# Bidirectional encoder trunk on one core: banks, places and order at the start of the retention stage

## The chip, the cores and the metric

The kernel runs on one core of one Trainium2 chip. The time is device microseconds of one execution; for the kernel before it is the median of three runs. Engines are named as in the profile: PE (TensorE matmul), PEld (its weight loads), DVE (VectorE), ACT (ScalarE), POOL (GpSimd), SP (SyncE, which issues most DMAs).

## The reference

Two groups of tokens (512 rows of 1024 each) pass through the same two layers, each of the form x + Mixer(RMSNorm(x)), and a final RMSNorm. The first mixer is differential attention, the second bidirectional retention. The part that matters here is the second:

```python
proj = h @ w_in                      # 1024 -> 2*1024 (q, k) + 2*2048 (values, gate)
q, k, v, gate = split(proj)
q, k = rotate(q), rotate(k) * RET_QK_DIM ** -0.5
o = retention(q, k, v, decay_fwd, True) + flip(retention(flip(q), flip(k), flip(v), decay_bwd, False))
o = rms_norm(o, subln_g, SUBLN_EPS).reshape(B, S, D_INNER) * silu(gate)
x = x + o @ w_out                    # 2048 -> 1024
```

There are 8 heads; q and k have 128 columns a head, values 256. One retention direction weights the scores q.k by a decay in the distance of the two rows, adds them up over the values of a chunk of 128 rows, and carries a state (k.v, decayed) from chunk to chunk. The kernel takes both directions together.

## The kernel before

**Arithmetic.** Every fp32 operand is split into a high and a low part (`hi_of` on ACT, `lo_of` on DVE, lines 469 to 473), and a product is made of three passes: high-high, high-low, low-high. The large matrix products use a scheme of seven products, named P1 to P7 and made in the order `SEQ` = P1, P2, P5, P6, P3, P7, P4; their partial results meet in three accumulators called x, y and z (line 42). P1, P5 and P2 open an accumulator; P6, P7 and P4 add to x, P3 adds to z. Between two of them ACT copies or DVE adds what stands in the accumulator so far, so P6 waits until P1 was copied, and so on.

**Stages.** The layer-1 projections, attention, the layer-2 projections (`projections`, line 855, over a list of `Unit`s), and then retention. The last layer-2 unit is a "wide" one that makes the values of heads 6 and 7; each of its products is four groups of twelve 128x256 matmuls (line 693). Its operands lie in numbered slots: P2's in slots 4 to 7, P1's in 0 to 3, P5's in 8 to 11, P6's in 26, 27, 14, 15. Its y accumulators take the two banks of tag `o` (5, 6), its z accumulators the two of tag `sc` (3, 4), its x accumulators two of the three of `pj` (0 to 2). `v_done` (line 813) splits each of its results and stores it to DRAM.

**Retention.** A block is a head of one group; there are 16, with four tiles of 128 rows each. `ahead(b, n)` prepares block b: `keys` (line 1594: split the keys, transpose them, L1603), two `score2` (L1623), `states` (L1643) and `queries`. Each takes a bank of tag `sc`. For each tile, `av2` (line 1669) makes the weighted sum with nine matmuls (L1679, L1683) in a bank of tag `o`; ACT squares it and takes a root (`norm_two`, lines 874 to 880), scales it (L896); PE turns it into the other half of the same bank (`turn_o`, L902); DVE multiplies it by the gate (`gate2`, L1336), which frees the bank. After two blocks of one group (a pair, counted p = 0 to 3, group g) the output product of that pair is owed: `out2` (line 1370) for two halves of rows r = 0, 1 with the seven products each (L1394), into the accumulators x (bank 0 for row 0, bank 7 for row 1), y (bank 1) and z (bank 2). `owe2` (line 1479) puts P1 of row 1 ahead of P4 of row 0. `evac_add` copies (L1433, L1450) or combines (L1438) the accumulators and adds the results to x in DRAM by an accumulating DMA from POOL (L970); the last pair adds to x in SBUF instead (`evac_last`, L1467). `w_split` (line 1313) loads one of the seven output weights of a pair (512 KB), from the weight matrix or from a sum `w1P` made earlier in DRAM, into one of two raw places and splits it (128x1024 on ACT and DVE).

**What sets the order.** Nothing runs when it is written. Every operation is put down in a plan with its engine, its cost, its reads and writes; `Plan.arrange` (line 141) then simulates the engines and writes out one order for each. PE takes operations in the order in which they were put down, within a window of 24; the others take what is due first, counted back from PE. A load counts as landed 2.0 + KB/200 us after its issue or later if the modelled bus is full (line 464), and is not issued more than 15 us before it is due. On the chip each engine then runs its list strictly in that order and waits at its head.

**The start of the retention stage** (lines 1701 to 1725). `LEFT` = 2 products of the last values unit (P7 and P4) are left when it begins. The loads of block 0 and its four `ahead` steps are put down, with the loads of block 1 after the first; the two products follow with tiles 0 and 1, and at tile 2 the seven `w_split`s of the first pair. Where everything lies is the table `LATE` (line 374): block 0 in the raw and staging places (raw0 to raw3, st0 to st2, os0), block 1 in slots 0 to 2 and 4 to 7.

**The last product** (P4 of row 1 of the last pair and group) is made in two halves of 256 columns (`part`, line 1397, matmuls L1401), each followed by its sum (L1408) and square (L1411).

Of the kernel before, what the change touches and what calls it, by code (L numbers as in the profile page):

```python
# [15 lines left out]
P = 128  # L16
S = 512
# [15 lines left out]
LEFT, LEFT1 = 2, 3  # L33
# [223 lines left out]
def trunk_kernel(  # L257
# [109 lines left out]
    def turns(kind, shape, dt=F32):  # L367
# [6 lines left out]
    LATE = dict(q0=["raw0"], k0=["raw1"], v0=["raw2", "raw3"], aT0=["st0", "st1"], kT0=["st2"], Z0=["os0"], sg0=["os1"], F0=[3],  # L374
                aT1=[0, 1], kT1=[2], Z1=["os2"], k1=[4], q1=[5], v1=[6, 7], AB=[8, 9, 10], sg1=[26], F1=[27], wa=[20], wb=[21], S4=[24],
                w=[11, 14, 15, 16, 17, 18, 19, "ws5", "ws6", 25, 12, 13, 22, 23],
                AS=["ws0", "ws1", "ws2", "ws3", "ws4"], O=["m1", "m2", "m3"], rt=["e0", "e1", "e2"], out=["e3", "e4", "e5", "e6", "e7"], R=["m0", "c3"],
                x=["raw0", "raw1", 20, 21, "raw2", "raw3", "os1", "os2"],
# [36 lines left out]
    BUFS = dict(pj=3, sc=2, o=2, tp=1, xs=1, x0=1, x1=1, y=1, z=1)  # L415
    BANKS = dict(pj=0, sc=3, o=5, tp=7, xs=3, x0=0, x1=7, y=1, z=2)
# [42 lines left out]
    def dma(out, in_, r, w, kb, eng=None, now=False):  # L459
# [4 lines left out]
        plan.op("SP" if eng is None else "ACT", 0.5, lambda: q.dma_start(out(), in_()), r, w, lands=2.0 + kb / 200.0,  # L464
                kb=kb, load=any(isinstance(k[0] if isinstance(k, tuple) else k, Buf) for k in w), now=now)

    last_store = [[]]
# [387 lines left out]
    def projections(units, early=None):  # L855

        if early is not None:
            units[2].early = early
        order = product_order(units)
        ready = 0  # L860
        for n, (u, op) in enumerate(order):
# [6 lines left out]
            u.product(op)  # L868
            u.evac(op)
            yield  # L870
# [148 lines left out]
    def units2(tab2):  # L1019
# [285 lines left out]
    def outputs(layer, xh, done):  # L1305
# [7 lines left out]
        def w_split(p, op):  # L1313

            src = w_d[layer, op, p] if (layer, op, p) in w_d else None
            t = late(("wa", "wb")[cnt_of.setdefault("raw", 0) % 2] + L, 0, [P, 2, S])
            cnt_of["raw"] += 1
            if src is None:
                e, i = W_BLOCK[op]
                dma(lambda: t.t, lambda: w_block(layer, p, e, i), [], [t], 512)  # L1320
            else:
                dma(lambda: t.t, lambda: src, [src], [t], 512)
            hi, lo = (late("w" + L, 2 * W_AT[op] + a, [P, 2, S], F32R) for a in range(2))
            hi_of(1024, lambda: hi.t, lambda: t.t, [t], [hi])
            lo_of(1024, lambda: lo.t, lambda: t.t, lambda: hi.t, [t, hi], [lo])
            wop[op] = (hi, lo)
# [43 lines left out]
        def out2(p, g, r, op):  # L1370
# [5 lines left out]
            if opens:  # L1376
                banks[which, r] = bank("xs" if which == "x" and ends and r else "x%d" % (r * layer) if which == "x" else which)
# [19 lines left out]
            def part(c):  # L1397
                at = slice(c * 256, c * 256 + 256)
                for i in range(2):
                    for n, (u, v) in enumerate(PASSES):  # L1400
                        nc.tensor.matmul(ps[:, at], pick(A[i], u), (hi, lo)[v][:, i, at], start=False,  # L1401
                                         stop=(i == 1 and n == 2), skip_group_check=True)
            if final:
                x, key = xh[g, 3][0]
                for c, own in enumerate(({}, {})):
                    at = slice(c * 256, c * 256 + 256)
                    pe(0.69, lambda c=c: part(c), [*A, hi, lo], [(ps, c)])
                    dve(256, lambda at=at: nc.vector.tensor_tensor(x()[:, at], x()[:, at], ps[:, at], op=ALU.add),  # L1408
                        [(ps, c), key], [own])
# [6 lines left out]
            pe(1.38, fn, [*A, hi, lo], [ps])  # L1416
# [153 lines left out]
    def fetch2(b):  # L1570
# [4 lines left out]
        dma(lambda: kf.t, lambda: k_src[h % 2], [k_src], [kf], 256)  # L1575
        dma(lambda: q.t.bitcast(F32), lambda: q_src[h % 2], [q_src], [q], 512)
        vt[b] = []
        for a in range(2):
# [3 lines left out]
                [src], [t], 512)  # L1582
# [7 lines left out]
    def decay(h):  # L1590
        t = Fs[h] = late(f"F{h % 2}", 0, [P, 2, S], F32R)
        dma(lambda: t.t.bitcast(F32), lambda: f_d[h][:], [f_d[h]], [t], 512)

    def keys(b):
# [4 lines left out]
        tp = bank("sc", "kT")  # L1599
# [14 lines left out]
    def score2(b, c):  # L1614
        h, g = blocks[b]
        s = bank("sc", "s2")
# [17 lines left out]
    def states(b):  # L1634
        z = bank("sc", "z2")
# [33 lines left out]
    def av2(b, t):  # L1669
        o = bank("o")  # L1670
# [31 lines left out]
    gate2, owe2, w_split = outputs(1, xh, final_norm)  # L1702
    fetch2(0)
# [107 lines left out]
```

## Time and profile before

| | us |
|---|---|
| median of three runs (lowest, highest) | 1833.79 (1831.55, 1835.36) |
| the profiled execution | 1829.8 |
| its span, first to last instruction | 1828.0 |
| PE busy | 1778.1 |
| DVE busy | 1485.2 |
| ACT busy | 1064.2 |

The profile is of one execution. Its page gives busy times, a row of 40 slices of the span, the chain of work that ended last, and groups of instructions by source line with the idle time before them. Views of the trace give the same for any stretch of time: busy time by windows, who waited for whom, the timeline. "L1679" is line 1679 of the kernel before. Tile names are those of the pools: `b` and `arena` are slots and places of the table above, `small` holds the keys of a block as loaded and the normed sums, `c` and `e` are copies and sums of accumulators.

### The profile page before, as it was taken

To read this page: it belongs to the slowest core of one execution; us is meant where nothing else is said; L and a number is where in the kernel's file an instruction comes from. 1 tells how busy PE (TensorE), PEld (TensorE's weight loads), DVE (VectorE), ACT (ScalarE), POOL (GpSimd) and SP (SyncE) were. 2 spreads that over 40 slices of the span, in tenths; PEclk is the share of its full clock that TensorE was granted. 3 is DMA by queue.
4 is the path that set the end of the run, shared out by engine and by line. 5 is a ranking of instruction groups with operands and counts; after the bars stand their busy time and mean duration, and the time that the engine had idled before them with its cause. 6 is when DMAs were issued, how large, how long until landed. Compare 5 with 4: busy or idle time off the path is not lost. (4 is left out here: it accounts for less than half of the span.)

```text
span 1828.0 us, 28378 instructions
## 1 busy us (share of the span) xinstructions
PE 1778.1 (97%) x10170; PEld 1532.2 (84%) x10170; DVE 1485.2 (81%) x2615; ACT 1064.2 (58%) x2278; POOL 240.6 (13%) x371
## 2 busy tenths in 40 slices
PE   7999999999999999999999999999999998999898
PEld 6988988988988878888888777989898897878776
DVE  7988888887888798888888897676766859778687
ACT  7644444444444486767677774444443458777674
POOL 3000000000000024443433100000000000121111
PEclk9999999999999999999999999999999999999999
DMA  8567667767766687878785457787765288889884
GB/s 289 166 182 200 199 187 200 213 174 204 209 175 185 237 294 220 244 232 249 233 246 185 139 168 235 208 243 209 228 195 168 98 273 266 232 221 257 225 244 138
DMA packets 197565, 387.04 MB, mean 212 GB/s; under 512 B 16432, under 2 KB 75440, under 8 KB 197296
## 3 DMA queue, kind: packets, MB, share of 16 engines
q1 hardware_dynamic: 174464, 342.95, 56.1%
q0 software_dynamic: 22528, 41.95, 14.4%
q8 instruction: 79, 1.29, 0.3%
q14 instruction: 62, 0.51, 0.1%
q10 hardware_dynamic: 432, 0.34, 0.1%
HBM read 250.96 MB, written 171.97 MB: 231 GB/s over the span
## 5 line engine op out<-in xcount | busy, mean ns | idle before, releaser
L645 PE MATMUL bank<-arena,ws 128*128 128x512 f32 x2202 | 527.2, 393 | 8.7 <-ACT ws L470 8.0
L645 PEld LDWEIGHTS bank<-arena,ws 128*128 128x128 f32 x2202 | 413.6, 189 | 100.6 <-ACT ws L470 8.0
L645 PE MATMUL bank<-b,ws 128*128 128x512 f32 x1170 | 290.8, 395 | 1.5 <-DVE e L722 1.5
L645 PEld LDWEIGHTS bank<-b,ws 128*128 128x128 f32 x1170 | 219.2, 188 | 52.7 <-DVE e L722 2.1
L1394 PE MATMUL bank<-b,b 128*128 128x512 f32 x794 | 212.6, 399 | 6.2 <-ACT c L1433 3.4
L470 ACT CAST ws<-st 128x512 fp32r<-128x512 f32 (+1 forms) x188 | 129.7, 694 | 135.5 <-PE bank L645 76.9
L693 PE MATMUL bank<-ws,arena 128*128 128x256 f32 x1728 | 205.0, 277 | 1.7 <-DVE e L803 1.7
L693 PEld LDWEIGHTS bank<-ws,arena 128*128 128x128 f32 x1728 | 201.4, 188 | 3.2 <-DVE e L803 1.9
L714 ACT COPY c<-bank 128x512 f32<-128x512 f32 x165 | 96.5, 585 | 174.7 <-PE bank L645 141.4
L473 DVE TENSOR_TENSOR ws<-st,ws 128x512 fp32r<-128x512 f32 (+1 forms) x188 | 145.4, 779 | 64.2 <-ACT ws L470 57.1
L1394 PEld LDWEIGHTS bank<-b,b 128*128 128x128 f32 x794 | 143.5, 188 | 35.6 <-ACT c L1433 3.9
L473 DVE TENSOR_TENSOR b<-b,b 128x512 fp32r<-128x512 f32 (+2 forms) x196 | 132.0, 686 | 19.0 <-ACT b L470 19.0
L722 DVE TENSOR_TENSOR e<-bank,c 128x512 f32<-128x512 f32 x165 | 113.7, 690 | 41.1 <-PE bank L645 34.2
L473 DVE TENSOR_TENSOR ws<-raw,ws 128x512 fp32r<-128x512 f32 (+1 forms) x143 | 109.8, 779 | 41.0 <-ACT ws L470 16.6
L970 POOL DMA_DIRECT2D x<-b x96 | 85.8, 903 | 376.6 <-DVE b L1438 253.4
L470 ACT CAST b<-b 128x512 fp32r<-128x512 f32 (+2 forms) x196 | 119.3, 621 | 24.6 <-DMA b<-w1P 8.1
L470 ACT CAST ws<-raw 128x512 fp32r<-128x512 f32 (+1 forms) x143 | 99.0, 698 | 56.5 <-PE bank L645 36.1
L693 PE MATMUL bank<-ws,b 128*128 128x256 f32 x960 | 118.8, 278 | 0.9 <-DVE e L722 0.9
L693 PEld LDWEIGHTS bank<-ws,b 128*128 128x128 f32 x960 | 114.7, 188 | 1.7 <-DVE e L722 1.1
L1243 ACT ACTIVATE b<-bank,nm 128x512 f32<-128x512 f32 x128 | 87.7, 687 | 35.0 <-DVE nm L1235 33.8
L1277 PE MATMUL bank<-arena 128*128 128x256 f32 x768 | 104.7, 286 | 0.2 <-DVE b L1336 0.2
L1227 PE MATMUL bank<-arena 128*128 128x512 f32 x384 | 101.8, 397 | 2.4 <-ACT b L1243 2.4
(213 smaller groups left out, 2847.4 us busy)
## 6 DMA issues: line engine op xcount, KB each, us to landing
qk<-os SPq DMA_DIRECT2D x160, 256.0 KB, 3.8
arena<-qk SPq DMA_DIRECT2D x72, 512.0 KB, 6.8
raw<-in_da_w_in_dram SPq DMA_DIRECT2D x64, 512.0 KB, 5.9
v<-os SPq DMA_DIRECT2D x60, 512.0 KB, 5.4
arena<-v SPq DMA_DIRECT2D x48, 512.0 KB, 5.5
x<-b POOLq DMA_DIRECT2D x96, 256.0 KB, 6.9
raw<-in_ret_w_in_dram SPq DMA_DIRECT2D x48, 512.0 KB, 6.2
g<-e SPq DMA_DIRECT2D x49, 256.0 KB, 5.9
```

What stands on the lines that cost most here:

```text
L470: act(n, lambda: nc.scalar.copy(dst(), src()), r, w)
L473: dve(n, lambda: nc.vector.tensor_tensor(dst(), src(), hi().bitcast(F32), op=ALU.subtract), r, w)
L645: nc.tensor.matmul(ps.t, a[u][0]()[:, k, :], bt[k][:, v, :], start=(opens and k == 0 and i == 0), stop=(k == 3 and i == 2), skip_group_che ...
L693: nc.tensor.matmul(ps[:, (t % 2) * 256:(t % 2) * 256 + 256], bt[k][:, v, t * P:(t + 1) * P], a[u][0]()[:, k, :], start=(opens and t % 2 == ...
L714: act(S, lambda c=c, ps=ps: nc.scalar.copy(c.t, ps.t), [ps], [c])
L722: dve(S, lambda e=e, ps=ps, c=c: nc.vector.tensor_tensor(e.t, ps.t, c.t, op=ALU.add), [ps, c], [e])
L970: plan.op("POOL", 1.0, lambda: nc.gpsimd.dma_start(out(), in_(), accum_op=ALU.add), r, w, lands=5.5, kb=kb, hold=hold)
L1227: nc.tensor.matmul(s.t, q[:, u, t * P:(t + 1) * P], k[:, v, :], start=(n == 0), stop=(n == 2))
L1243: act(840, lambda j=j, s=s, m=m: nc.scalar.activation(p[:, j, :], s.t, AF.Exp, bias=m.t, accum_out=sm[:, j:j + 1]), [s, m], [(p, j), (sm, j)])
L1277: nc.tensor.matmul(o[:, 0:256], aT[:, a, j * P:(j + 1) * P], v[b][:, j, :], start=(n == 0), stop=(n == 11))
L1394: nc.tensor.matmul(ps.t, pick(A[i], u), (hi, lo)[v][:, i, :], start=(opens and n == 0), stop=(n == 5), skip_group_check=True)
```

## The change

- Weighted sums take banks 5, 6 and 7 by a new tag `o2`. Bank 7 serves as x accumulator of row 1 only in the last pair and group; before that both rows use bank 0, and `owe2` puts row 0 wholly ahead of row 1.
- Block 0's keys, scores and states take banks of `o2`, not of `sc`. `LEFT` is 5: P5, P6, P3 are put down between the steps of `ahead(0)`, P7 at tile 1 and P4 at tile 4. Three of the first pair's weight splits (P1, P2, P5) are put down there too, P6 and P3 at tile 1, P7 and P4 at tile 4, with raw places of their own (`wc`).
- Blocks 0 and 1 change places in `LATE`; the loads of blocks 0 and 1, their decay tables and the first weights are no longer held back to 15 us before they are due (`soon`), and block 1's loads are put down after `ahead(0, 2)`, not `ahead(0, 0)`.
- For every DMA put down from the retention stage on, the plan counts 3.5 us more until it lands (`behind`).
- Three of the last unit's four pairs of value sums, before the change two, are stored from slots (9, 10 and 26; before 9, 10, 11, 14), not from the rotating `os` tiles. The first two x tiles of the last pair lie in e7, c0 to c2, and the results of the output products turn over four tiles, not five.
- `projections` prepares the next product's weights before it yields, not after.
- The last product is made in one piece of 512 columns; its sum and square are still made in halves.

```diff
-LEFT, LEFT1 = 2, 3
+LEFT, LEFT1 = 5, 3
...
-    LATE = dict(q0=["raw0"], k0=["raw1"], v0=["raw2", "raw3"], aT0=["st0", "st1"], kT0=["st2"], Z0=["os0"], ...
-                aT1=[0, 1], kT1=[2], Z1=["os2"], k1=[4], q1=[5], v1=[6, 7], ... wa=[20], wb=[21], ...
+    LATE = dict(q1=["raw0"], k1=["raw1"], v1=["raw2", "raw3"], aT1=["st0", "st1"], kT1=["st2"], Z0=["os0"], ...
+                aT0=[0, 1], kT0=[2], Z1=["os2"], k0=[4], q0=[5], v0=[6, 7], ... wa=[20], wb=[21], wc=["st0", "st1", "os2", 21, 20, 21, 20], ...
...
-    BUFS = dict(pj=3, sc=2, o=2, tp=1, xs=1, x0=1, x1=1, y=1, z=1)
-    BANKS = dict(pj=0, sc=3, o=5, tp=7, xs=3, x0=0, x1=7, y=1, z=2)
+    BUFS = dict(pj=3, sc=2, o=2, o2=3, tp=1, xs=1, x0=1, x1=1, y=1, z=1)
+    BANKS = dict(pj=0, sc=3, o=5, o2=5, tp=7, xs=3, x0=0, x1=7, y=1, z=2)
...
-        plan.op("SP" if eng is None else "ACT", 0.5, lambda: q.dma_start(out(), in_()), r, w, lands=2.0 + kb / 200.0,
-                kb=kb, load=any(...), now=now)
+        plan.op("SP" if eng is None else "ACT", 0.5, lambda: q.dma_start(out(), in_()), r, w, lands=2.0 + kb / 200.0 + behind[0],
+                kb=kb, load=not soon and any(...), now=now)
...
-                o = slot(next(free), [P, 2, S]) if free and i else os_t()
+                o = slot(next(free), [P, 2, S]) if free and (i or g) else os_t()
...
-                             iter((9, 10, 11, 14)) if h == NH - 2 else None))
+                             iter((10, 26, 9, 10, 9, 10)) if h == NH - 2 else None))
...
-                banks[which, r] = bank(... else "x%d" % (r * layer) if which == "x" else which)
+                banks[which, r] = bank(... else "x%d" % (r * (layer and (p, g) == (LASTP, 1))) if which == "x" else which)
...
-            order = rows[0][:-1] + rows[1][:1] + rows[0][-1:] + rows[1][1:] if layer or (p, g) == (LASTP, 1) else rows[0] + rows[1]
+            order = rows[0][:-1] + rows[1][:1] + rows[0][-1:] + rows[1][1:] if (p, g) == (LASTP, 1) else rows[0] + rows[1]
...
-        tp = bank("sc", "kT")
+        tp = bank("sc" if b else "o2", "kT")
...
-        o = bank("o")
+        o = bank("o2")
...
+    behind[0] = 3.5
     fetch2(0)
     decay(0)
...
+    EARLY = ((), (), ("P1",), ("P2", "P5"))
     for n in range(4):
         ahead(0, n)
-        if n == 0:
+        for op in EARLY[n]:
+            w_split(0, op, True)
+        if n < 3:
+            step(proj)
+        if n == 2:
             fetch2(1)
     for i in range(N2 + 2):
-        if i < LEFT:
-            step(proj)
-        elif i == LEFT:
-            run(proj)
-            for op in SEQ:
-                w_split(0, op)
+        if i in (1, 4):
+            run(proj) if i > 1 else step(proj)
+            for op in SEQ[5:] if i > 1 else SEQ[3:5]:
+                w_split(0, op, True)
```

More of the change, by code (lines that the diff above doesn't have):

```diff
@@ L457, in pe, with dma @@
         plan.op("PE", cost, fn, r, w)
-    def dma(out, in_, r, w, kb, eng=None, now=False):
+    def dma(out, in_, r, w, kb, eng=None, now=False, soon=False):
         q = eng or nc.sync
@@ L463, in dma @@
             last_store[0] = [w[0]]
-        plan.op("SP" if eng is None else "ACT", 0.5, lambda: q.dma_start(out(), in_()), r, w, lands=2.0 + kb / 200.0,
-                kb=kb, load=any(isinstance(k[0] if isinstance(k, tuple) else k, Buf) for k in w), now=now)
-    last_store = [[]]
+        plan.op("SP" if eng is None else "ACT", 0.5, lambda: q.dma_start(out(), in_()), r, w, lands=2.0 + kb / 200.0 + behind[0],
+                kb=kb, load=not soon and any(isinstance(k[0] if isinstance(k, tuple) else k, Buf) for k in w), now=now)
+    last_store, behind = [[]], [0.0]
     def hi_of(n, dst, src, r, w):
@@ L860, in projections @@
         ready = 0
-        for n, (u, op) in enumerate(order):
+        for n in range(len(order) + 1):
             while ready < len(order):
@@ L867, in projections @@
                 ready += 1
-            u.product(op)
-            u.evac(op)
-            yield
+            if n:
+                yield
+            if n < len(order):
+                u, op = order[n]
+                u.product(op)
+                u.evac(op)
     def norm_two(o):
@@ L1376, in out2 @@
             if opens:
-                banks[which, r] = bank("xs" if which == "x" and ends and r else "x%d" % (r * layer) if which == "x" else which)
+                banks[which, r] = bank("xs" if which == "x" and ends and r else "x%d" % (r * (layer and (p, g) == (LASTP, 1))) if which == "x" else which)
             ps, (hi, lo) = banks[which, r], wop[op]
@@ L1396, in fn @@
                         n += 1
[L1397 to L1402, printed above, removed]
+            pe(1.38, fn, [*A, hi, lo], [ps])
             if final:
@@ L1406, in out2 @@
                     at = slice(c * 256, c * 256 + 256)
-                    pe(0.69, lambda c=c: part(c), [*A, hi, lo], [(ps, c)])
                     dve(256, lambda at=at: nc.vector.tensor_tensor(x()[:, at], x()[:, at], ps[:, at], op=ALU.add),
-                        [(ps, c), key], [own])
+                        [ps, key], [own])
                     ss, jk = col(1, "ssf", 4), turns("out", [P, 256])
@@ L1574, in fetch2 @@
         kf = kfs[b] = Buf(plan, "kf", 1, lambda i: small[:, 512:1024], lambda i: (-512, 0))
-        dma(lambda: kf.t, lambda: k_src[h % 2], [k_src], [kf], 256)
-        dma(lambda: q.t.bitcast(F32), lambda: q_src[h % 2], [q_src], [q], 512)
+        dma(lambda: kf.t, lambda: k_src[h % 2], [k_src], [kf], 256, soon=b < 2)
+        dma(lambda: q.t.bitcast(F32), lambda: q_src[h % 2], [q_src], [q], 512, soon=b < 2)
         vt[b] = []
@@ L1581, in fetch2 @@
             dma(lambda a=a, t=t: t.t.bitcast(F32), lambda a=a, src=src: src[a].rearrange("p (t e) -> p t e", t=NT),
[L1582 removed]
+                [src], [t], 512, soon=b < 2)
             vt[b].append(t)
@@ L1615, in score2 @@
         h, g = blocks[b]
-        s = bank("sc", "s2")
+        s = bank("sc" if b else "o2", "s2")
         q, k = qk[b, 0], qk[b, 1]
@@ L1634, in states @@
     def states(b):
-        z = bank("sc", "z2")
+        z = bank("sc" if b else "o2", "z2")
         kT, v_ = kTs[b], vt[b]
```

32 lines of the change are left out of this document (18 added, 14 removed).

## The prediction

> **What bounds the kernel now.** I read the page first, then the busy time in windows, then the waits of TensorE (PE) and ScalarE (ACT) in the last stage, then the chain that ended last, then single stretches of the timeline.
>
> ```profile
> span 1828.0 us, 28378 instructions
> ...
> PE 1778.1 (97%) x10170; PEld 1532.2 (84%) x10170; DVE 1485.2 (81%) x2615; ACT 1064.2 (58%) x2278; POOL 240.6 (13%) x371
> ```
>
> PE is the bound: 1828.0 - 1778.1 leaves 49.9 us without a matmul, so a change that removes no PE work can only win from these. The question is which of them lie in the stage that is edited. The windows view gives for each stretch PE, weight load, VectorE (DVE), ACT and POOL busy, the clock, the DMA share and GB/s; I cut it at the attention stage, the last values products, the first two retention blocks, the rest of the retention stage in two parts, and the tail.
>
> ```profile
> 655.00:980.00 325.00, 320.18 (x1881) 273.85 (x1882) 287.97 (x588) 236.15 (x597) 126.55 (x214) 1.00 0.82 245
> 1440.00:1489.00 49.00, 49.00 (x344) 45.24 (x343) 28.48 (x36) 25.95 (x52) 0.00 (x0) 1.00 0.49 155
> 1489.00:1535.00 46.00, 40.06 (x304) 36.83 (x302) 39.22 (x76) 37.17 (x93) 0.92 (x1) 1.00 0.90 313
> 1535.00:1600.00 65.00, 64.50 (x404) 56.94 (x404) 53.68 (x112) 49.91 (x128) 10.45 (x12) 1.00 0.82 227
> 1600.00:1800.00 200.00, 187.00 (x1123) 160.16 (x1122) 158.94 (x326) 142.43 (x368) 33.62 (x41) 1.00 0.83 231
> 1800.00:1828.00 28.00, 19.14 (x87) 14.80 (x86) 19.37 (x34) 9.04 (x25) 4.20 (x9) 0.94 0.30 114
> ```
>
> PE stands idle 46 - 40.06 = 5.9 us while the stage starts, 0.5 us in 1535 to 1600, 13.0 us in 1600 to 1800, and 8.9 us in the tail, where the last products, sums and stores follow each other. So 19.4 us are within reach of edits to this stage. Just before it, in 1440 to 1489, DVE is busy only 58% of the time and ACT 53%; in the next 46 us DVE is at 85% and ACT at 81%. Who ends PE's waits: the first row is of the window 1489 to 1535, the next three of 1535 to 1810 (columns: sum, times, longest).
>
> ```profile
> PE bank L1679 <- DVE b L1336: 3.1, 3, 1.4
> ```
> ```profile
> PE bank L1679 <- DVE b L1336: 5.4, 10, 1.3
> PE bank L1394 <- ACT c L1433: 3.4, 2, 2.2
> PE bank L1643 <- DMA arena<-v: 2.9, 3, 1.5
> ```
>
> L1679 is the weighted sum of a tile; what it waits for is L1336, the gating that reads the turned sum out of the same bank two tiles before. With two banks a late gating stops PE at once. Why the gating is late shows in ACT's waits (1500 to 1800), the landing times of the same window, and two pieces of the chain:
>
> ```profile
> ACT arena L470 <- DMA small<-qk: 16.1, 6, 3.8
> ACT b L470 <- DMA small<-qk: 12.2, 5, 5.2
> ACT b L470 <- DMA b<-w1P: 8.1, 4, 2.9
> ACT arena L470 <- DMA b<-in_ret_w_out_dram: 2.2, 1, 2.2
> ```
> ```profile
> x<-b POOLq DMA_DIRECT2D x48, 256.0 KB, 7.5
> b<-w1P SPq DMA_DIRECT2D x16, 512.0 KB, 5.4
> b<-in_ret_w_out_dram SPq DMA_DIRECT2D x10, 512.0 KB, 10.3
> small<-qk SPq DMA_DIRECT2D x13, 256.0 KB, 7.3
> ```
> ```profile
> 1605.38 10.02 DMA b<-w1P
> ...
> 1622.77 8.72 DMA small<-qk
> ```
>
> ACT stood 38.6 us at the head of its queue before a split whose load had not landed, with square roots, copies out of the banks and splits queued behind. The planner counted a landing at 2 + KB/200 us, so 3.3 us for the keys (256 KB) and 4.6 for a weight (512 KB); the chip took 7.3 and 5.4 to 10.3. The order was written for loads that land earlier than they do.
>
> **The change, part by part.** All terms are against the profiled execution, 1829.8 us (span 1828.0). The median of the timed runs, 1833.8, lies 4.0 above it; I carry that over.
>
> *Start of the stage* (five products left instead of two, block 0 on the banks of the sums, three of seven weight splits during the products).
>
> ```profile
> 1465.61 11.05 PE L693 MATMUL bank<-ws,arena 128*128 128x256 f32 x96
> ...
> 1505.16 0.88 PE L1679 MATMUL bank<-b,b 128*128 128x256 f32 x6
> 1505.88 0.52 PE L1683 MATMUL bank<-b,b 128*128 128x256 f32 x3
> ...
> 1510.15 0.98 PE L1679 MATMUL bank<-b,b 128*128 128x256 f32 x6 [1.38 <-DVE b L1336]
> ```
> ```profile
> L1603 PE MATMUL bank<-ident,small x64: 272/272/328, 1487.4 to 1761.8; 128*128 128x128 f32 x64
> ```
> ```profile
> 1461.55 0.34 SPq L464 DMA_DIRECT2D b<-qk  x1
> ```
> ```profile
> L473 DVE TENSOR_TENSOR b<-b,b 128x512 fp32r<-128x512 f32 x58 | 39.2, 685 | 5.7 <-ACT b L470 5.7
> L470 ACT CAST arena<-b 128x1024 fp32r<-128x1024 f32 x16 | 16.8, 1049 | 2.2 <-DMA b<-in_ret_w_out_dram 2.2
> L473 DVE TENSOR_TENSOR arena<-b,arena 128x1024 fp32r<-128x1024 f32 x12 | 14.7, 1224 | 5.3 <-ACT arena L470 5.3
> ```
>
> The 96 matmuls from 1465.61 are P2 and P5 of the last unit; P2 ends half way, at 1465.6 + 11.05 / 2 = 1471.1. Block 0 moves to the places of P2's operands (4 to 7), so its q, k and v, which SP issued from 1461.55 on, now can't be issued before 1471.1: later, not sooner. With a 256 KB landing of 7.3 us its first matmuls stand at about 1478.5, still 9 us before the 1487.4 of the key transposes now, because the banks that P5 to P3 hold (3 and 4) are no longer the ones it needs. Block 1 takes the raw and staging places, free earlier. In those 9 us PE has P5, P6 and P3, which ran without retention work beside them. What moves ahead of 1489 on DVE: block 0's ten 512-wide operations, 10 x 0.685 = 6.9 us, and three weight splits, 3 x 1.224 = 3.7 us; together 10.6 us, which would take DVE in 1489 to 1535 from 39.2 to 28.6 of 46. On ACT three splits are 3 x 1.049 = 3.1 us. The first values sums stored through arena slots instead of the rotating staging tiles cost no instruction. PE loses nothing by holding five products: they fill what was idle. The moved loads (three weights of 512 KB, and block 1's reads) pass the values stores on SP, and a store that waits for its split holds them; that is why I do not take all of the 5.9 us. Bounds: gain 0 (loads land as late as now) to 5.9. I take 4.5.
>
> *Third bank, and 3.5 us more landing in the plan* (1535 to 1800). The sums turn over banks 5, 6, 7, so a gating may be one tile later, about 4.6 us (64 tiles from 1505 to 1800); the longest wait was 1.4 us. The plan's landings become 6.8 us (256 KB) and 8.1 (512 KB), close to the 7.3 and 5.4 to 10.3 measured, so loads are asked for earlier and the split that needs one stands later in ACT's queue. Of the waits 5.4 + 3.4 + 2.9 = 11.7 us listed above I take 60%, 7.0 us. Bounds: 0 (ACT still blocked) to the whole 13.5 us of 1535 to 1800.
>
> *Restart.* In an unbroken stream the next group starts 1505.88 - 1505.16 = 0.72 us after one that lasts 0.88, so 0.16 us of drain is hidden; each wait pays it on top. The quoted rows count 3 + 10 + 2 + 3 = 18 waits; I let 14 go: 14 x 0.16 = 2.2 us. Bounds 0 and 2.9.
>
> *One bank less for the output products.* Bank 7 was the x bank of row 1. Now both rows use bank 0 (outside the last group) and follow each other: P7 to P4, P4 to the next row's P1, twice for each of 7 groups, where only P7 to P4 of row 1 was back to back before. That is 3 x 7 = 21 added handovers. One that exists already:
>
> ```profile
> 1559.61 1.55 PE L1394 MATMUL bank<-b,b 128*128 128x512 f32 x6
> ...
> 1561.78 0.68 DVE L1438 TENSOR_TENSOR b<-c,bank 128x512 f32<-128x512 f32 x1
> ...
> 1562.74 1.65 PE L1394 MATMUL bank<-b,b 128*128 128x512 f32 x6
> ...
> 1564.98 0.60 ACT L1450 COPY b<-bank 128x512 f32<-128x512 f32 x1
> ```
>
> P7 ends at 1561.16, DVE reads it until 1562.46, P4 starts at 1562.74: 1.6 us from product to product, and no idle time stands before P4, since a weighted sum and transposes fill it. That work lies between two products everywhere in this stage. Cover gone, a handover costs 1.6 us, so the bounds are 0 and 21 x 1.6 = 33 us. I take 0.1 each, 2.1 us, by this row and by the 0.5 us idle of 1535 to 1600. Out tiles fall from five to four: a row makes four in about 17 us (16 rows in 275), an addition lands in 7.5, so nothing.
>
> *The last product in one piece.*
>
> ```profile
> 1819.49 1.65 PE L1401 MATMUL bank<-b,b 128*128 128x256 f32 x12 [1.30 <-DVE b L1467]
> ...
> 1820.35 0.75 DVE L1696 SCALAR_TENSOR_TENSOR b<-b,rsf,sin 128x512 f32<-128x512 f32 x1
> 1821.17 0.76 DVE L1408 TENSOR_TENSOR b<-b,bank 128x256 f32<-128x256 f32 x2
> ```
>
> The halves bought nothing: DVE was in L1696 until 1821.10, PE ended at 1821.14, and the first half sum began at 1821.17. Six 512-wide matmuls after a wait take the same 1.65 us (1562.74 above). Cost 0.1, bounds 0 to 0.7.
>
> *Weights prepared one step earlier in program order, and a new order by the planner everywhere else.* No instruction more; 50 to 1440 has no wait that this aims at. Zero, bounds -1 to +2.
>
> Sum: -4.5 - 7.0 - 2.2 + 2.1 + 0.1 = -11.5 us. 1829.8 - 11.5 = 1818.3; with the 4.0 of the median, 1822.3, rounded to **1822**; its own range 1816 to 1828.
>
> **The rivals.**
>
> *Transfers set the pace, so waits only move.* The DMA engines are busy 0.82 to 0.90 of this stage at 227 to 313 GB/s. If the late landings are a queue in front of the engines, loads asked for earlier land no earlier, ACT still stands 38.6 us, and the third bank merely hands the wait to the next in line. Left are the start, its three restarts (0.5) and the handovers: -4.5 - 0.5 + 2.1 + 0.1 = -2.8, so 1831.0. Against it: the landings of 7 to 10 us are each shorter than the 15 us by which the plan may run ahead, and the loads have buffers. The Trainium skill, page "DMA: Bandwidth & Descriptors", section "Issuing engines are not separate DMA queues", says that all transfers run on the same 16 engines and interleave whoever issues them; by that rule an earlier request takes its bandwidth from the stores and additions beside it, and the time would be this rival's. The trace agrees as far as the shares above go; that a load's landing grows when others are issued sooner, no row shows. Chance 0.20.
>
> *The single x bank becomes the bound.* The 13.7 us won (4.5 + 7.0 + 2.2) are gone when a handover costs 13.7 / 21 = 0.65 us. At 1.0 us, an evacuation queued behind one 1.05 us weight split, it is +21.0 - 13.7 + 0.1 = +7.4: 1841.2, slower than before. For it: DVE and ACT are at 79% and 71% in 1600 to 1800, so such queueing is common. Against: the attention stage runs its rows on a single x bank, with DVE at 89% and ACT at 73%, and loses only 4.8 us in 325, though it has more other PE work between two products. Chance 0.15.
>
> *Everything goes.* All 19.4 us of idle time and the 2.9 of restarts, no handover paid: 1833.8 - 22.3 = 1811.5. Chance 0.10.
>
> **How the numbers follow.** Forecast 0.55, everything 0.10, transfers 0.20, x bank 0.15. The range 1811 to 1837 reaches from the second case into the last, and leaves out most of that (0.12) and a few hundredths of other mishaps. What a measurement of this kernel can tell from no change is 0.2%, 3.7 us. Faster than 1830.1: 0.55 + 0.10 + 0.08 of the transfers case = 0.73; within: 0.11 of the transfers case + 0.03 of the x bank's = 0.14; slower than 1837.5: 0.12 of the x bank's + 0.01 = 0.13.
>
> **What would show it.** Right: PE idle in the first 46 us of the stage under 2 us, L1679 no longer first among PE's waits, ACT's waits for the keys under 15 us. Wrong: output products waiting on the copies and sums that read bank 0 for over 10 us in all (x bank); ACT's waits for loads unchanged with landings above 10 us (transfers); new waits among the last products before 1500 (loads and splits that block the values sums).

## The result and the profile after

The changed kernel takes 1815.7 us (median of four, 1814.6 to 1817.5) against 1834.0 for the kernel before: ratio 0.9903, 95% interval 0.9886 to 0.9920. That is faster by 18 us, and 6 us faster than the 1822 forecast. Its profiled execution took 1815.84 us. From its page:

```profile
span 1814.1 us, 28383 instructions
...
PE 1777.3 (98%) x10164; PEld 1535.9 (85%) x10164; DVE 1485.1 (82%) x2615; ACT 1063.3 (59%) x2278; POOL 239.9 (13%) x371
```

The busy time is the same to within 1 us on every engine (the weight loads, PEld, take 3.7 us more); 1814.1 - 1777.3 leaves 36.8 us without a matmul where there were 49.9. The windows of the last stage, in the same columns as before (PE, weight load, DVE, ACT, POOL, clock, DMA share, GB/s):

```profile
1489.00:1535.00 46.00, 45.73 (x352) 43.60 (x351) 44.07 (x88) 39.54 (x104) 1.26 (x2) 1.00 0.83 278
1535.00:1600.00 65.00, 65.00 (x414) 58.06 (x413) 54.36 (x117) 49.77 (x130) 13.60 (x16) 1.00 0.90 244
1600.00:1800.00 200.00, 191.67 (x1117) 165.62 (x1116) 159.95 (x324) 137.97 (x356) 32.10 (x41) 0.97 0.79 221
```

PE's idle time went from 5.9 to 0.3 us in the first stretch, from 0.5 to 0 in the second, and from 13.0 to 8.3 in the third, where the granted clock is now 0.97 instead of 1.00. The waits of PE (1489 to 1800), and below them those of ACT for loads (1490 to 1800):

```profile
PE bank L1402 <- ACT b L1451: 4.0, 1, 4.0
PE bank L1402 <- DVE b L1468: 2.3, 2, 2.0
PE bank L1402 <- ACT c L1434: 1.6, 2, 1.4
PE bank L905 <- ACT small L899: 0.4, 2, 0.2
PE bank L1680 <- DVE b L1344: 0.3, 1, 0.3
```
```profile
ACT arena L470 <- DMA small<-qk: 8.1, 3, 4.7
...
ACT b L470 <- DMA b<-in_ret_w_out_dram: 4.2, 3, 2.0
...
ACT b L470 <- DMA b<-w1P: 1.0, 2, 0.8
```

and the landing of the keys (median, 1500 to 1800):

```profile
small<-qk SPq DMA_DIRECT2D x13, 256.0 KB, 7.2
```

L1680 is what L1679 was: the weighted sums wait 0.3 us in all. ACT stands 13.3 us before loads that have not landed, against 38.6. What is left is nearly all of one kind: an output product (L1402, before L1394) that waits for its accumulator.

To see where the time came from, I cut both executions at three events: the end of the last paired product (L645), the first output product, and the last matmul. In the kernel before:

```profile
1462.82 2.95 PE L645 MATMUL bank<-b,ws 128*128 128x512 f32 x12
...
1526.43 1.55 PE L1394 MATMUL bank<-arena 128*128 128x512 f32 x6
```

and after:

```profile
1461.58 2.95 PE L645 MATMUL bank<-b,ws 128*128 128x512 f32 x12
...
1469.83 0.60 PE L1604 MATMUL bank<-ident,small 128*128 128x128 f32 x4
...
1489.85 0.96 PE L1680 MATMUL bank<-arena 128*128 128x256 f32 x6
...
1520.41 1.55 PE L1402 MATMUL bank<-arena 128*128 128x512 f32 x6
...
1800.38 4.54 PE L1402 MATMUL bank<-b,b 128*128 128x512 f32 x18
```

Up to the last paired product: 1465.8 and 1464.5, so -1.3 us. From there to the first output product ("start" below): 1526.43 - 1465.77 = 60.7 and 1520.41 - 1464.53 = 55.9, -4.8. From there to the last matmul ("stage"): 1821.14 - 1526.43 = 294.7 and 1804.92 - 1520.41 = 284.5, -10.2. From there to the end of the span ("tail"): 6.9 and 9.2, +2.3. Together -14.0, the difference of the spans (13.9). Of the stage's 10.2 us, 8.2 are idle time of PE (294.7 - 278.2 = 16.5 before, 284.5 - 276.2 = 8.3 after). The key transposes of block 0 stand at 1469.8, 17.6 us earlier than the 1487.4 of before; the prediction said 1478.5.

### The profile page after: what moved, and what is told of

The parts are those of the page before. It is cut to its first block, busy times and chain, and to the rows that moved or that the text cites. A ratio compares the mean times of both kernels' runs of the same rounds, so it can differ in the third digit from the quotient of the medians.

```text
span 1814.1 us, 28383 instructions
## 1 busy us (share of the span) xinstructions
PE 1777.3 (98%) x10164; PEld 1535.9 (85%) x10164; DVE 1485.1 (82%) x2615; ACT 1063.3 (59%) x2278; POOL 239.9 (13%) x371
## 4 chain that ended last, share of the span: by engine, by line
PE 83%; DMA 7%; DVE 4%; issue 3%; ACT 2%; POOL 1%; SPq 0%; ACTq 0%; DVEq 0%; POOLq 0%
PE bank L645 40%; PE bank L693 16%; PE bank L1402 12%; PE bank L1280 4%; PE bank L1230 4%; PE bank L1680 2%; DMA b<-in_ret_w_out_dram 2%; DMA b<-w0P 1%; DMA b<-in_da_w_out_dram 1%; PE bank L905 1%; PE bank L1265 1%; PE bank L1644 1%; PE bank L1624 1%; DMA raw<-in_ret_w_in_dram 1%; PE bank L1684 1%
## 5 line engine op out<-in xcount | busy, mean ns | idle before, releaser
L645 PE MATMUL bank<-arena,ws 128*128 128x512 f32 x2202 | 527.0, 393 | 7.5 <-ACT ws L470 7.1
L645 PEld LDWEIGHTS bank<-arena,ws 128*128 128x128 f32 x2202 | 413.2, 188 | 99.5 <-ACT ws L470 7.1
L645 PE MATMUL bank<-b,ws 128*128 128x512 f32 x1170 | 290.7, 395 | 0.3 <-DVE e L722 0.3
L645 PEld LDWEIGHTS bank<-b,ws 128*128 128x128 f32 x1170 | 219.2, 188 | 51.3 <-DVE e L722 0.5
L1402 PE MATMUL bank<-b,b 128*128 128x512 f32 x800 | 213.1, 398 | 2.3 <-ACT c L1434 1.6
L1402 PEld LDWEIGHTS bank<-b,b 128*128 128x128 f32 x800 | 145.3, 188 | 32.4 <-ACT c L1434 2.0
```

What stands on the lines that cost most here:

```text
L645: nc.tensor.matmul(ps.t, a[u][0]()[:, k, :], bt[k][:, v, :], start=(opens and k == 0 and i == 0), stop=(k == 3 and i == 2), skip_group_che ...
L1402: nc.tensor.matmul(ps.t, pick(A[i], u), (hi, lo)[v][:, i, :], start=(opens and n == 0), stop=(n == 5), skip_group_check=True)
```

## The experiments

My theory named three causes that add up: the start, the third bank, and the plan's allowance for landings. The change can be cut along these lines, so I ran all combinations, each planned anew ("start changed" stands for all of the change but the bank, with its x bank and order of rows, and the allowance; the last product in one piece is part of it), then the x bank by itself, other sizes of the allowance, and the keys by another way. "Ratio" is against runs of the kernel before on the same chip, with its 95% interval; the last four columns are the segments above, and the sum of the first two, in us, from one profiled execution each.

| kernel | start changed | third bank | allowance | median us | ratio (interval) | start, us | stage, us | start + stage, us | tail, us |
|---|---|---|---|---|---|---|---|---|---|
| before | - | - | 0 | 1833.7 | 1 | 60.7 | 294.7 | 355.4 | 6.9 |
| e1_land | - | - | 3.5 | 1815.2 | 0.9904 (0.9887 to 0.9922) | 59.1 | 283.2 | 342.3 | 6.9 |
| e12_land175 | - | - | 1.75 | 1826.6 | 0.9963 (0.9951 to 0.9976) | 65.5 | 280.6 | 346.1 | 6.9 |
| e2_bank | - | yes | 0 | 1827.9 | 0.9977 (0.9961 to 0.9993) | 61.4 | 286.9 | 348.3 | 8.2 |
| e4_xbank_only | - | x bank only | 0 | 1836.9 | 1.0020 (1.0007 to 1.0034) | 63.0 | 297.1 | 360.1 | 7.8 |
| e3_bank_land | - | yes | 3.5 | 1814.3 | 0.9903 (0.9882 to 0.9924) | 60.4 | 278.7 | 339.1 | 6.8 |
| e7_start | yes | - | 0 | 1837.0 | 1.0025 (1.0010 to 1.0041) | 57.5 | 302.2 | 359.7 | 8.0 |
| e5_no_land | yes | yes | 0 | 1817.8 | 0.9911 (0.9892 to 0.9931) | 56.8 | 285.4 | 342.2 | 7.9 |
| e6_no_bank | yes | - | 3.5 | 1807.8 | 0.9858 (0.9837 to 0.9879) | 56.4 | 278.7 | 335.1 | 8.0 |
| e10_no_bank_land5 | yes | - | 5.0 | 1809.1 | 0.9863 (0.9849 to 0.9878) | 61.3 | 273.6 | 334.9 | 7.2 |
| e9_land_xbank | yes | x bank only | 3.5 | 1812.8 | 0.9886 (0.9872 to 0.9899) | 56.4 | 282.6 | 339.0 | 7.9 |
| changed | yes | yes | 3.5 | 1815.7 | 0.9903 (0.9886 to 0.9920) | 55.9 | 284.5 | 340.4 | 9.2 |
| e8_land6 | yes | yes | 6.0 | 1817.7 | 0.9914 (0.9895 to 0.9933) | 56.8 | 283.2 | 340.0 | 10.1 |
| e11_two_keys | - | - (second place for the keys) | 0 | 1826.7 | 0.9958 (0.9943 to 0.9973) | 58.4 | 294.8 | 353.2 | 6.9 |

Every one of these gives the planner other input, and it orders the whole kernel anew: the end of the last paired product lies between 1462.6 and 1468.9 in them, though nothing before it was meant to change. So differences of a few us between medians need not come from the edit that names the kernel. The segments leave out what happened before the stage, but each row is one execution, between 3.9 us below the median of its kernel (before) and 4.4 us above it (e6), and the first output product moves too; so start and stage together say more than either. The medians come from three series, in which the kernel before took 1833.7 (e1 to e4), 1832.0 (e5 to e8) and 1833.5 us (e9 to e12): compare the ratios.

One more figure can be set against all these times: how long ACT stood before splits whose load had not landed (1500 to 1800, as for the 38.6 us above). It is 38 to 39 us in the kernel before, e4 and e7 (1833.7 to 1837.0); 18 to 28 us in e11, e12 and e2 (1826.6 to 1827.9); and 14.3 us or less in e1, the changed kernel, e9, e6, e3, e10 and e8 (1807.8 to 1817.7). One kernel does not fit: e5 has 28.3 us and takes 1817.8. Inside the last group the waits set no order: e8 has none and takes 1817.7, e6 has 7.7 us and takes 1807.8.

### The allowance alone

```diff
+    behind[0] = 3.5
     fetch2(0)
     decay(0)
```
(with `lands=2.0 + kb / 200.0 + behind[0]` in `dma`, on the kernel before)

> The kernel before with the 3.5 us landing allowance in the plan and nothing else. Theory (late splits at the head of ScalarE's queue delay the gatings): 1826 to 1829 us, ScalarE's waits for the keys in the retention stage down from 28.3 us to under 15. Rival A (the third bank did it, the plan's landings do nothing): 1834 within 2 us, waits for the keys unchanged. Rival B (the allowance did nearly everything): under 1823.

Measured: 0.9904, as much as the whole change. Rival B holds and the sizes of my theory don't. ACT's waits, the waits of the sums for the gating (1489 to 1800), and the windows:

```profile
ACT b L470 <- DMA small<-qk: 10.8, 5, 3.5
...
ACT b L470 <- DMA b<-w1P: 3.5, 2, 2.8
```
```profile
PE bank L1679 <- DVE b L1336: 6.9, 10, 2.1
```
```profile
1489.00:1535.00 46.00, 41.83 (x309) 39.47 (x308) 39.92 (x80) 38.48 (x99) 0.00 (x0) 0.96 0.82 285
...
1600.00:1800.00 200.00, 196.42 (x1169) 170.20 (x1168) 169.49 (x341) 145.52 (x375) 33.74 (x44) 1.00 0.83 233
```

Waits for the keys fell from 28.3 to 10.8 us and PE's idle time in 1600 to 1800 from 13.0 to 3.6, with two banks for the sums. The waits for the gating did not go: 6.9 us are left of 8.5, since they fell from 5.0 to 1.7 in 1600 to 1800 and rose before 1535. The waits of the output products in 1600 to 1800 fell from 5.7 to 0.7. Start and stage together are 13.1 us shorter; another 3.2 us of this profile lie ahead of the stage, where nothing was meant to change. The start stretch still idles 4.2 us: that part the allowance does not reach.

### Half the allowance

```diff
-    behind[0] = 3.5
+    behind[0] = 1.75
```
(against e1)

> The kernel before with half the allowance, 1.75 us. Theory (an error in the plan's landings that shrinks in proportion): 1822 to 1827, keys waits between 28 and 11 us. Rival (a threshold, or a lucky order at 3.5): 1834, or 1815 already.

Measured 1826.6, 0.9963: between, as the theory has it. ACT's waits:

```profile
ACT b L470 <- DMA small<-qk: 10.1, 5, 2.9
ACT b L470 <- DMA b<-w1P: 10.1, 3, 6.0
...
ACT arena L470 <- DMA small<-qk: 5.1, 3, 2.3
```

Keys 15.2 us, between 28.3 and 10.8. Start and stage together take 346.1 us, between 355.4 and 342.3 too; the stage alone does not (280.6, e1 283.2), as the first output product comes later here. A lucky order at 3.5 alone is made unlikely by this and by e3, e6 and e10; that every new order brings some us of its own is not ruled out.

### The keys by another way

```diff
-        kf = kfs[b] = Buf(plan, "kf", 1, lambda i: small[:, 512:1024], ...)
+        kf = kfs[b] = late("kf", 0, [P, S]) if b % 2 else Buf(plan, "kf", 1, lambda i: small[:, 512:1024], ...)
```
(`kf=["e7"]`, and `out` without e7)

> The kernel before with two places for the keys as loaded (the second is the fifth place of the output results, so these turn over four as in the change); the plan's landings as before. Theory (the waits at the head of ScalarE's queue for the keys are the cause, the allowance is one way to be rid of them): keys waits from 30 us to under 10, and 1820 to 1827 us. Rival (the allowance works by another order of everything, and the keys are a symptom): 1832 or more though the keys waits fall.

Measured 1826.7, 0.9958. The keys no longer appear among ACT's waits (1500 to 1800); another load does:

```profile
ACT b L470 <- DMA b<-w1P: 15.3, 5, 6.3
...
ACT arena L470 <- DMA b<-w1P: 1.6, 2, 1.2
```

With the plan's landings still wrong, the next load takes their place at the head of the queue: the weights' waits went from 8.1 to 16.9 us. In one place the trace shows the whole path, from ACT to PE:

```profile
1766.37 1.04 ACT L470 CAST b<-b 128x1024 fp32r<-128x1024 f32 x1 [6.25 <-DMA b<-w1P]
...
1767.32 0.47 ACT L896 ACTIVATE small<-bank,crr 128x256 f32<-128x256 f32 x1
...
1767.84 0.69 PE L902 MATMUL bank<-ident,small 128*128 128x128 f32 x2 [4.75 <-ACT small L896]
```

ACT stands 6.25 us before a weight. The scaling behind it in the queue (L896) had its last input, `crr`, from DVE by 1761.18, and PE stands 4.75 us until it is done. The median fell by 0.42%, so the late keys cost time by themselves; this profile does not show where the gain lies, since its start and stage are only 2.2 us shorter than before. The allowance treats all loads at once, which fits its gain of more than twice as much.

### The third bank

```diff
-        o = bank("o")
+        o = bank("o2")
```
(`o2` is banks 5, 6 and 7; row 1's x accumulator lies in bank 0 outside the last group, by the two lines shown for e4 below)

> The kernel before with three banks for weighted sums and one x bank outside the last group, nothing else. Theory: 1828 to 1832 us, the waits of the weighted sums for the gating gone (8.5 us before) but half of it back as output products that wait. Rival A (third bank did it): 1820 to 1825. Rival B (allowance): 1834 to 1837, since the one x bank costs 2 us.

Measured 1827.9, 0.9977: the theory's time, a little under its lower end. The sums hardly wait for the gating any more (0.3 us in 1489 to 1800); in their place PE waits for the transposes' input and, as expected, for output products:

```profile
PE bank L902 <- ACT small L896: 5.5, 6, 1.5
...
PE bank L1394 <- DVE b L1467: 1.7, 2, 1.6
PE bank L1394 <- DVE b L1438: 1.7, 3, 1.2
```

L902 needs what ACT scales, and ACT still stood 28.1 us before loads: the late queue now stops PE one step further on.

The price of bank 7 alone, on the kernel before:

```diff
-                ... "x%d" % (r * layer) if which == "x" else which)
+                ... "x%d" % (r * (layer and (p, g) == (LASTP, 1))) if which == "x" else which)
...
-            order = ... if layer or (p, g) == (LASTP, 1) else rows[0] + rows[1]
+            order = ... if (p, g) == (LASTP, 1) else rows[0] + rows[1]
```

> The kernel before with one x bank outside the last group and rows one after the other, weighted sums still in two banks: the price of the 21 added handovers alone. Theory: +2 us, 1834 to 1838. Rival (the x bank is a bound that something else pays for): 14 us or more, 1848 and above.

Only the x bank and the order of the rows, sums in two banks: 1.0020, so +3.7 us (1.3 to 6.2) for 21 handovers, 0.18 us each. The rival of 14 us is out. Taken with e2, the third bank earns 8 us (1.0020 to 0.9977) and pays 4 for its place.

Both, `behind[0] = 3.5` and the bank, on the kernel before:

```diff
+    behind[0] = 3.5
...
-        o = bank("o")
+        o = bank("o2")
```

> The kernel before with the third bank and the landing allowance together, start of the stage as before. Theory: the two add up, 1821 to 1824 us, and what is left to the changed kernel (1815.7) is the start, 6 to 8 us. If the two take the same waits, the same time as the better of them alone.

Third bank on top of the allowance: 0.9903 against 0.9904. The bank does take the waits of the sums (6.9 us in e1, 0.3 here), but others stand in their place: transposes for ACT's scaling (3.3 us, L902) and output products (4.8 us, L1394). So on top of the allowance it moves waits, and earns nothing that the medians show. In this one profile start and stage are 3.2 us shorter than in e1 (339.1 against 342.3), and they begin 5.5 us later (1468.1 against 1462.6); what of either comes from the new order is not shown.

The changed kernel with one line less:

```diff
-    behind[0] = 3.5
```

> The changed kernel without the 3.5 us landing allowance. Theory: 1821 to 1824 us, ScalarE again waits over 20 us for the keys. Rival A (third bank did it): 1816 within 2. Rival B (allowance did nearly everything): 1826 or more.

The whole change without the allowance: 0.9911, within the noise of the whole (0.9903). Rival A's number, and still not its theory, since e1 got there without the bank. ACT waits 14.6 us for the keys, not the over 20 that I expected, and 28.3 us for loads in all. So the allowance is not the only way to this time: the start alone loses 0.25% (e7), the bank alone gains 0.23% (e2), and the two together gain 0.89%. Why they are worth so much more together than alone stays open.

The changed kernel with the banks of before:

```diff
-    BUFS = dict(pj=3, sc=2, o=2, o2=3, tp=1, ...)
+    BUFS = dict(pj=3, sc=2, o=2, o2=2, tp=1, ...)
...
-                ... "x%d" % (r * (layer and (p, g) == (LASTP, 1))) if which == "x" else which)
+                ... "x%d" % (r * layer) if which == "x" else which)
...
-            order = ... if (p, g) == (LASTP, 1) else rows[0] + rows[1]
+            order = ... if layer or (p, g) == (LASTP, 1) else rows[0] + rows[1]
```

> The changed kernel with two banks for the weighted sums and the x bank of row 1 back, old order of the rows. Theory: 1819 to 1822 us, with the weighted sums waiting for the gating again by 3 to 5 us. Rival A (third bank): 1826 or more. Rival B (allowance): 1816 or a little less, since the handovers of the one x bank go.

The whole change without the third bank: 1807.8, 0.9858, better than any number I had put down and clear of the changed kernel's interval. (Its profiled execution, 1812.2 us, is the slowest of its six.) Its waits on PE and its window:

```profile
PE bank L1680 <- DVE b L1344: 2.7, 6, 0.7
...
PE bank L1402 <- DVE b L1468: 0.7, 1, 0.7
```
```profile
1489.00:1535.00 46.00, 44.42 (x344) 42.44 (x343) 42.58 (x83) 39.28 (x97) 0.92 (x1) 1.00 0.87 295
...
1600.00:1800.00 200.00, 196.11 (x1164) 169.54 (x1163) 170.04 (x341) 144.50 (x371) 33.81 (x44) 1.00 0.82 231
```

The sums wait again, but 2.7 us in all, and the output products that wait 7.9 us in the changed kernel (4.0 + 2.3 + 1.6) wait 0.7. One more kernel splits the difference, the changed one with only the third bank taken out:

```diff
-    BUFS = dict(pj=3, sc=2, o=2, o2=3, tp=1, ...)
+    BUFS = dict(pj=3, sc=2, o=2, o2=2, tp=1, ...)
```

> Start and landing allowance as changed, weighted sums in two banks, but one x bank outside the last group and rows one after the other (bank 7 left unused until then). Without any of the bank change this kernel took 1807.8, with all of it 1815.7. Theory (the third bank has nothing left to win once loads are planned rightly, and the 8 us are the added handovers): 1814 to 1818. Rival (the third bank itself costs, by a worse order): 1806 to 1810.

With the x bank given up but no third bank: 0.9886, a little under the lower end of the expected times and above the rival's. The 8 us between e6 and the changed kernel are thus some 5 us of handovers (0.9858 to 0.9886) and some 3 us (0.9886 to 0.9903) that come with the bank itself. The handovers show in start and stage too (335.1 to 339.0), though the intervals of e6 and e9 just overlap. Those of e9 and the changed kernel overlap further, and their start and stage differ by 1.4 us; whether the bank costs anything by itself stays open.

### The start alone

The allowance and the bank (with the x bank and the rows, as in e6) taken out of the changed kernel, the rest kept:

```diff
-    behind[0] = 3.5
...
-    BUFS = dict(pj=3, sc=2, o=2, o2=3, tp=1, ...)
+    BUFS = dict(pj=3, sc=2, o=2, o2=2, tp=1, ...)
```

> The changed kernel with neither the third bank nor the allowance: the start of the stage alone (five products left, places, early splits, loads not held back). Theory: 1826 to 1829 us, the first 46 us of the stage under 2 us idle, later stretches as before. Rival (the start only moves waits to the first output products): 1833 to 1835.

Measured 1.0025: slower, the one outcome that neither theory nor rival gave. The first stretch does what it should, the later ones lose more:

```profile
1489.00:1535.00 46.00, 44.88 (x350) 42.72 (x349) 42.27 (x83) 38.36 (x95) 0.92 (x1) 1.00 0.84 287
1535.00:1600.00 65.00, 61.72 (x379) 53.34 (x378) 49.14 (x102) 46.23 (x120) 10.51 (x12) 1.00 0.77 208
1600.00:1800.00 200.00, 184.22 (x1097) 157.25 (x1096) 155.28 (x319) 139.76 (x360) 32.78 (x39) 0.99 0.80 224
```
```profile
ACT b L470 <- DMA small<-qk: 18.4, 7, 4.7
ACT arena L470 <- DMA small<-qk: 14.8, 5, 5.1
...
ACT b L470 <- DMA b<-w1P: 5.6, 3, 2.8
```

Idle 1.1 us in the first 46, where there were 5.9, then 3.3 and 15.8 where there were 0.5 and 13.0; ACT waits 33.2 us for keys, against 28.3. With the allowance the same start gains: e6 against e1, 0.9904 to 0.9858, some 8 us. Why the start alone loses 7.5 us in the stage, I did not find out.

### More allowance

```diff
-    behind[0] = 3.5
+    behind[0] = 6.0      # e8, on the changed kernel; 5.0 in e10, on e6
```

> The changed kernel with an allowance of 6.0 us in place of 3.5. Its longest wait left, 4.0 us at 1633, is a key load that took 12.3 us where the plan counted 6.8. Theory: that wait goes, 1810 to 1813 us. Rival (the engines of the DMA queues are the bound; earlier loads only wait longer, and places are held longer): 1816 or more.

On the changed kernel 6.0 us brings nothing (0.9914): the rival's number, but not its cause, since the keys landed in 6.2 us (median; 7.2 with 3.5) and ACT waited for no load in 1500 to 1800. The 4.0 us wait is gone, others of PE came: one wait for a split on DVE (2.6 us) and five for DVE's sums out of the accumulators (3.3 us).

> Start as changed, two banks for the sums, two x banks, and an allowance of 5.0 us in place of 3.5. Theory: the allowance has done its work at 3.5, so 1805 to 1810. If loads asked for still earlier crowd each other, 1812 or more.

On e6 5.0 us gives 1809.1, the same within the intervals: 5 us less in the stage, 5 us more in the start, and the two together alike (335.1, 334.9). **e6_no_bank, the change without its third bank, has the lowest time of the study**, level with e10; against the kernel before it gains 1.4%, where the whole change gains 1.0%.

## Why the prediction was right or wrong

**Direction and range: right.** The three signs named in advance came: under 2 us of idle time in the first 46 (0.3), L1679 no longer first among the waits, ACT's waits for keys under 15 us (8.1). The forecast's own range, 1816 to 1828, was missed by 0.3 us, and 1815.7 lies nearer to the rival that everything goes (1811.5) than to the sum (1822.3). That the sum came this close is in part luck: it added up parts that, run by themselves and in pairs, do not add up.

**From profile to median: wrong, and most of the 6 us.** I carried 4.0 us from the profiled execution to the median. The sum itself said 1818.3 for the profiled execution, which took 1815.84. But the profiled execution of before (1829.8) was faster than each of its timed runs (1831.55 at the least), while that of after lies in the middle of its own.

**The start, -4.5 and three restarts: right in size, here, and not in its working.** The segment became 4.8 us shorter, and the idle time of the first 46 us fell by 5.7. But DVE was to be relieved: 10.6 us ahead of 1489, and 28.6 us busy in 1489 to 1535 instead of 39.2. It was busy 3.0 us more in 1440 to 1489 (31.45 against 28.48) and 44.07 us in 1489 to 1535: no relief, more work in both, and the first weighted sum stands at 1489.85 instead of 1496.51. The step that put the first matmuls at 1478.5 held for q and the values, which were issued at 1470.82 and 1471.55; the keys as loaded lie in `small`, not in P2's slots, were asked for at 1327.57 already, and the transposes read them there right behind P2. Nor does this part stand by itself: alone it ends 0.25% slower (e7), 3.2 us shorter in the start segment and 7.5 us longer in the stage.

**Third bank and allowance, -7.0 and restarts, as one term: the size was short, and the split that I left open is the lesson.** The stage gained 10.2 us in the changed kernel. The allowance alone is worth 11.5 in the stage and 17.6 in the time (e1); the third bank alone 4.2 net; both together no more than the allowance. The diagnosis ahead of the term, an order written for loads that land earlier than they do, is borne out: correcting it gains the whole 1.0% on the kernel before (e1), half of it gains less (e12), and in all kernels but e5 the time goes, by the groups above, with ACT's waits for loads. It is not the whole account: inside the changed kernel the same allowance is worth nothing that can be measured (e5), and each correction also gave the planner another order. The bank's waits, which the sum took as something to win, moved elsewhere when the bank was there (e2, e3). No run separates the restarts from the waits.

**The single x bank, +2.1: nearly right** without the allowance (e4, +3.7, 1.3 to 6.2), some 5 us on top of start and allowance (e9). The rival that it becomes the bound at 1 us a handover is out. Of the 8.3 us that PE still idles in the changed kernel's stage, 7.9 are output products that wait for an accumulator; the longest of these waits, 4.0 us, goes back to a late key load (last section).

**The last product in one piece, +0.1 (0 to 0.7): wrong.** The tail after the last matmul grew from 6.9 to 9.2 us:

```profile
1804.96 0.42 DVE L1410 TENSOR_TENSOR b<-b,bank 128x256 f32<-128x256 f32 x1 [0.71 <-PE bank L1402]
...
1805.30 0.74 DVE L1697 SCALAR_TENSOR_TENSOR b<-b,rsf,cos 128x512 f32<-128x512 f32 x1
...
1805.96 0.74 DVE L1697 SCALAR_TENSOR_TENSOR b<-b,rsf,sin 128x512 f32<-128x512 f32 x1
...
1806.62 0.41 DVE L1410 TENSOR_TENSOR b<-b,bank 128x256 f32<-128x256 f32 x1
```

PE ends at 1804.92, the first half sum follows at once, and the second stands behind two scalings of other rows. I had priced the matmuls and not the order that the planner would choose behind them. The kernels with one piece have tails of 7.2 to 10.1 us, those with two pieces 6.8 to 8.2; the edit was not run by itself, so its own price stays open.

**Transfers set the pace (0.20): out.** Loads asked for earlier did land in time: the median landings hardly moved (keys 7.3 and 7.2 us) and ACT's waits fell to a third. The additions to x beside them landed in 7.3 us against 7.5 (medians, 1500 to 1800), so these did not become later. The share of the DMA engines went from 0.90 to 0.83, from 0.82 to 0.90 and from 0.83 to 0.79 in the three stretches. The Trainium skill, page "DMA: Bandwidth & Descriptors", section "Issuing engines are not separate DMA queues", says that all transfers share 16 engines whoever issues them; no run here contradicts that, but the time that the prediction drew from it (1831.0) did not come.

## What to carry to other kernels

When an engine with a strict queue is found standing before a load, look at what the order was planned with before adding buffers behind it: here one constant, set to the landing times of the trace, was worth as much on the kernel before as the whole edit. Remedies need not add up: the allowance and the bank together gave no more than the allowance, the start and the bank far more than their sum. So try each alone and in pairs before paying for both; with start and allowance in place, the bank and the handovers it brings cost more than they earned. And when a planner orders everything anew, compare segments between fixed events, in more than one execution, since places that no one touched move by some us.

## What the runs showed of the hardware

A wait of PE can cost more than its length, when the clock falls behind it. In the changed kernel the longest wait, 4.0 us, came from one key load that took 12.33 us (chain of the changed kernel):

```profile
1623.35 12.33 DMA small<-qk
...
1637.04 2.93 PE bank L1402 x6
```

The windows after it, and those around a wait of 2.0 us (the figure before the DMA share is the granted clock):

```profile
1637.00:1640.00 3.00, 2.96 (x8) 2.29 (x9) 1.90 (x5) 1.69 (x4) 0.86 (x1) 0.50 0.44 57
1640.00:1641.00 1.00, 1.00 (x6) 1.00 (x5) 0.57 (x2) 0.71 (x2) 0.00 (x0) 0.50 0.55 96
1641.00:1650.00 9.00, 9.00 (x56) 8.11 (x55) 4.90 (x11) 4.92 (x12) 0.86 (x1) 0.95 0.39 84
```
```profile
1778.50:1780.50 2.00, 0.01 (x1) 0.01 (x1) 2.00 (x5) 0.00 (x0) 0.00 (x0) 1.00 1.03 379
1780.50:1781.80 1.30, 1.30 (x6) 1.07 (x7) 1.22 (x2) 0.00 (x0) 0.00 (x0) 1.00 0.96 370
1781.80:1785.20 3.40, 3.40 (x10) 2.65 (x9) 1.03 (x2) 0.72 (x2) 0.00 (x0) 0.52 0.10 38
```

After the 4.0 us wait the clock is 0.50 for 4 us and a group of six matmuls takes 2.93 us instead of 1.65; half of 4 us and 5% of 9 us are some 2.5 us more, an estimate from these windows. After the 2.0 us wait it fell to 0.52 too, 1.3 us into the work that followed, for 3.4 us. The Trainium skill, page "TensorE: Matmul & The Clock Gate", section "What's actually happening", has the clock at half rate after an idle window of about 3.4 us; the first case agrees with it, and the second fell after a wait well under that. In the kernel before, a wait of 2.2 us that ended at 1617 left the clock at 1.00 (window 1600 to 1800). So the length of a single wait does not tell by itself whether the clock falls.
